# Three 256-column matmuls in place of a 512 and a 256 for channel-major weight tiles, with a one-step eviction

## The chip, the cores and the metric

The kernel runs on one core of one Trainium2 chip. The metric is device microseconds of one execution; the time of a kernel is the median of its runs. Engines are named as in the profile: PE is TensorE's matmul, PEld its weight load, DVE VectorE, ACT ScalarE, POOL GpSimd, SP SyncE, which issues the transfers.

## The reference

One decoder layer over 256 positions of width 2048, in float32:

```python
h = rmsnorm(x, norm1_g)
qkv, z, b_raw, a_raw, u_raw, v_raw, ga_raw, gb_raw = split(h @ w_in)
qkv = silu(causal_dwconv(qkv, dn_conv_w))          # 4 taps, along time, per channel
y_a = rmsnorm(gated_delta_rule(q, k, v, ...)) * silu(z)
y_b = gelu(u_raw) * spatial_mix(layernorm(gelu(v_raw)))
x = x + (sigmoid(ga_raw) * (y_a @ w_branch_a) + sigmoid(gb_raw) * (y_b @ w_branch_b)) @ w_out
h2 = rmsnorm(x, norm2_g)
gate = causal_dwconv(h2 @ ffn_w_gate, ffn_conv_w) + ffn_conv_b   # 3 taps
x = x + (silu(gate) * (h2 @ ffn_w_up)) @ ffn_w_down               # D_FF = 5632
return rmsnorm(x, final_norm_g)
```

## The kernel before

All products run in float32r, split for precision. A weight block arrives in SBUF by one transfer of 1 MB (`w_raw`), and `split` makes two float32r tiles of it: ACT casts the block to `w_hi` (L123), and DVE subtracts to get `w_lo`, the remainder (L124). The activations are split the same way and kept side by side in one tile: columns 0 to 255 are the high part of the 256 positions, columns 256 to 511 the low part. A product is hi x hi + lo x hi + hi x lo; the smallest term is left out.

There are two kinds of product. In the token-major kind (`tok_steps`, L157 to L159, and the down projection, L863 to L865) the weights stream as the moving operand, and the activations are loaded as stationary weights: three matmuls per tile, of 512 columns (346 and 348 in ps_u). In the channel-major kind (`chan_group`, L186 and L189) the weight tile is the stationary operand, 128 x 128, and the 256 positions move, so that channels lie on partitions and the causal convolution can run along the free axis. It is used in two stages: the six groups of qkv (ps_qkv) and the 22 groups of gate and up in the feed-forward part (ps_gu). A group is 512 output channels, that is, four row blocks in four PSUM banks (two from pool acc, two from aux, each pool with four banks, so that two groups fit), accumulated over 16 blocks of the inner dimension. The weights come in chunks of two inner blocks, through a ring of four buffers for each of hi and lo; a chunk is 8 weight tiles.

`chan_evict` takes a pair of row blocks out of PSUM into `dst` (`pre` in qkv, `gu` in gate-up), adds the two halves and multiplies by `rrow`, the reciprocal root of the normalisation for each position. Behind it come the convolution (ACT and DVE), the silu (ACT) and, in gate-up, the product with up into `y_f` on POOL.

A scheduler of the framework orders each engine's instructions, and puts work of one stage in between that of another where it expects room. So at the end of the qkv stage, PE already runs matmuls of the gates (ps_gate), and the preparation of the delta rule starts: ps_g on PE, exponentials on ACT (L489 to L495), the product g_r on POOL (L498), which ps_gr on PE (L500) waits for. g_r waits for the last silu of v (`v_t`, L454). ACT loads a table when it changes from silu to the exponential or back.

Of the kernel before, what the change touches and what calls it, by code (L numbers as in the profile page):

```python
# [9 lines left out]
F32 = mybir.dt.float32  # L10
F32R = mybir.dt.float32r
AF = mybir.ActivationFunctionType
ALU = mybir.AluOpType
# [3 lines left out]
P = 128  # L17
D = 2048
T = 256
NT = T // P  # L20
NK = D // P
# [77 lines left out]
def decoder_kernel(ctx: ExitStack, tc: tile.TileContext, a: dict):  # L99
    nc = tc.nc  # L100
# [7 lines left out]
    acc = ctx.enter_context(tc.tile_pool(name="acc", bufs=4, space=PSUM))  # L108
    aux = ctx.enter_context(tc.tile_pool(name="aux", bufs=4, space=PSUM))

    def bank(pool, name):
        return pool.tile([P, 512], F32, name=name, tag="bank")
# [14 lines left out]
    def source(name, g):  # L127

        cols = GROUPS[name]
        return a["w_" + name], sum(n for _, n in cols[:g]), cols[g][1]  # L130

    def stream(src, n_k, before=None):

        flat, start, width = src
        for k0 in range(0, n_k, 4):
            raw = wraw.tile([P, 4, 512], F32, name="w_raw", tag="raw")
            at = P * (start * n_k + k0 * width)
            block = flat[at : at + 4 * P * width].rearrange("(p k n) -> p k n", p=P, n=width)

            n, m = (4, 2) if not before else (2, 2) if k0 else (1, 1)  # L140
            for j in range(0, 4, n):
                if before:
                    before(k0 + j, n)
                nc.sync.dma_start(raw[:, j : j + n, 0:width], block[:, j : j + n, :])
            for j in range(0, 4, m):
                yield k0 + j, m, *split(raw[:, j : j + m, 0:width], [P, m, 512], "w")

    def tok_steps(x, src, n_k, name, before=None):

        ps = [bank(acc, f"{name}{t}")[:, 0 : src[2]] for t in range(NT)]  # L150
        for k0, n, hi, lo in stream(src, n_k, before):
            for t in range(NT):
                for j in range(n):
                    k = k0 + j
                    xh = x[:, k, t * P : (t + 1) * P]
                    xl = x[:, k, T + t * P : T + (t + 1) * P]
                    nc.tensor.matmul(ps[t], lhsT=xh, rhs=hi[:, j, :], start=(k == 0), stop=False)  # L157
                    nc.tensor.matmul(ps[t], lhsT=xh, rhs=lo[:, j, :], start=False, stop=False)  # L158
                    nc.tensor.matmul(  # L159
                        ps[t], lhsT=xl, rhs=hi[:, j, :], start=False, stop=(k == n_k - 1)  # L160
                    )
            yield
        return ps

    def finish(steps):

        while True:
            try:
                next(steps)
            except StopIteration as e:  # L170
                return e.value

    def tok_group(*args, **kw):
        return finish(tok_steps(*args, **kw))

    def chan_group(x, src, name):


        ps = [bank(pool, name) for pool in (acc, acc, aux, aux)]
        for k0, n, hi, lo in stream(src, NK):  # L180
            for m in range(4):
                ms = slice(m * P, (m + 1) * P)
                for j in range(n):
                    k = k0 + j
                    xk = x[k // 8][:, k % 8, :] if isinstance(x, list) else x[:, k, :]
                    nc.tensor.matmul(  # L186
                        ps[m], lhsT=hi[:, j, ms], rhs=xk, start=(k == 0), stop=(k == NK - 1), skip_group_check=True
                    )
                    nc.tensor.matmul(  # L189
                        ps[m][:, 0:T], lhsT=lo[:, j, ms], rhs=xk[:, 0:T], start=False, stop=(k == NK - 1),  # L190
                        skip_group_check=True,
                    )
        return ps

    def chan_evict(pool, dst, ps):

        lo = pool.tile([P, 2, T], F32, name="ev_lo", tag="ev_lo")
        for i in range(2):
            nc.scalar.copy(lo[:, i, :], ps[i][:, T:])
            nc.vector.tensor_tensor(dst[:, i, :], ps[i][:, 0:T], lo[:, i, :], op=ALU.add)  # L200
        nc.gpsimd.tensor_tensor(dst, dst, bc(rrow, 1, 2), op=ALU.mult)  # L201

    def split_stat(dst_hi, dst_lo, src, scale=None):

# [55 lines left out]
    def bc(ap, axis, n):  # L260

        shape = list(ap.shape)
        shape.insert(axis, n)
        return ap.unsqueeze(axis).broadcast_to(shape)

    def rsqrt_small(dst, src, scale):

        n = src.shape[-1]
        v = small.tile([P, n], F32, name="rs_v", tag=f"rs_v{n}")
        nc.vector.tensor_scalar(v, src, scalar1=scale, scalar2=EPS, op0=ALU.mult, op1=ALU.add)  # L270
        nc.gpsimd.tensor_tensor(dst, v, neg_half[:, 0:n], op=ALU.pow)

    def row_broadcast(dst, col):

        ps = bank(aux, "ps_row")
        for t in range(NT):
            dg = small.tile([P, P], F32, name="dg", tag="dg")
            nc.vector.tensor_scalar(
                dg, cm["ident"], scalar1=col[:, t : t + 1], scalar2=None, op0=ALU.mult
            )  # L280
            nc.tensor.matmul(ps[:, t * P : (t + 1) * P], lhsT=cm["ones"], rhs=dg, start=True, stop=True)
        nc.scalar.copy(dst, ps[:, 0:T])
# [14 lines left out]
    rrow = const.tile([P, T], F32, name="rrow")  # L297
# [11 lines left out]
    with tc.tile_pool(name="sg", bufs=1) as sg:  # L309
# [28 lines left out]
        for c, (start, width) in enumerate(GROUPS["bau"]):  # L338
            ps = tok_group(x_h, source("bau", c), NK, "ps_u_")
# [77 lines left out]
    def qkv_group(col):  # L417

        ps = chan_group(x_h, source("qkv", col // 512), "ps_qkv")
        for b in range(2):  # L420
            pre = tmp.tile([P, 2, 4 + T], F32, name="pre", tag="pre")
            nc.gpsimd.memset(pre[:, :, 0:4], 0.0)
            chan_evict(tmp, pre[:, :, 4:], ps[2 * b : 2 * b + 2])
            for m in range(2):
                ct = col // P + 2 * b + m
                cv = tmp.tile([P, T], F32, name="cv", tag="cv")
                nc.scalar.activation(cv, pre[:, m, 4:], AF.Copy, scale=cw[:, 4 * ct + 3 : 4 * ct + 4])
                for j in range(3):
                    nc.vector.scalar_tensor_tensor(
                        cv, pre[:, m, 1 + j : 1 + j + T], cw[:, 4 * ct + j : 4 * ct + j + 1], cv,  # L430
                        op0=ALU.mult, op1=ALU.add,
                    )
                yield ct, cv
# [360 lines left out]
    tmp = ctx.enter_context(tc.tile_pool(name="p3t", bufs=2))  # L794
# [4 lines left out]
    for c in range(4):  # L799
        cs = slice(512 * c, 512 * (c + 1))  # L800
        ps = finish(wo_steps if c == 0 else tok_steps(x_m, source("out", c), NK, "ps_wo"))
# [4 lines left out]
        for q in range(2):  # L806
            ps_t = bank(aux, "ps_x2t")
            for i in range(2):
                for t in range(NT):
                    k = 4 * c + 2 * q + i  # L810
# [3 lines left out]
            for i in range(2):  # L814
                k = 4 * c + 2 * q + i
# [4 lines left out]
    for f in range(0, NF, 2):  # L820
        ps = chan_group(x_h2, source("gu", f // 2), "ps_gu")
        if f == 0:
            rstd2 = const.tile([P, NT], F32, name="rstd2")
            s2 = const.tile([P, NT], F32, name="s2")
            nc.vector.tensor_reduce(s2, ss2, axis=AX.X, op=ALU.add)
            rsqrt_small(rstd2, s2, 1.0 / D)
            row_broadcast(rrow, rstd2)
        for i in range(2):
            ff = f + i
            gu = tmp.tile([P, 2, 384], F32, name="gu", tag="gu")[:, :, 0 : 4 + T]  # L830
            nc.gpsimd.memset(gu[:, 0, 0:4], 0.0)
            chan_evict(tmp, gu[:, :, 4:], ps[i::2])
            cv = tmp.tile([P, T], F32, name="f_cv", tag="f_cv")
            nc.scalar.activation(
                cv, gu[:, 0, 4:], AF.Identity, scale=fcw[:, 3 * ff + 2 : 3 * ff + 3], bias=fcb[:, ff : ff + 1]
            )
            for j in range(2):
                nc.vector.scalar_tensor_tensor(
                    cv, gu[:, 0, 2 + j : 2 + j + T], fcw[:, 3 * ff + j : 3 * ff + j + 1], cv,
                    op0=ALU.mult, op1=ALU.add,  # L840
                )
            nc.scalar.activation(cv, cv, AF.Silu)
            nc.gpsimd.tensor_tensor(y_f[ff // 32][:, ff % 32, :], cv, gu[:, 1, 4:], op=ALU.mult)
# [39 lines left out]
    for t in range(NT):  # L883
        for c in range(4):

            for h in range(1 if c < 3 else 2):
                w = 512 if c < 3 else 256
                lo = 512 * c + w * h
# [82 lines left out]
```

## Time and profile before

| | us |
|---|---|
| median of 3 runs | 1443.18 (1441.46 to 1444.53) |
| profiled execution | 1441.32 |
| its span, first to last instruction | 1439.6 |
| PE busy | 1418.4 |
| DVE, ACT, POOL busy | 898.0, 719.1, 241.9 |
| qkv stage, first to last start of a ps_qkv matmul | 106.2 to 241.2 |
| gate-up stage, the same of ps_gu | 701.7 to 1191.6 |

Rows of the trace give a start in microseconds from the span's start, a duration, the engine, the line of the kernel and the operands. Rows of groups give the count after x, then the total busy time and the mean of one in ns, then the idle time of the engine just before them. Rows of waits give the total, the number of times and the longest. A matmul's recorded duration includes its way through the array, so that the pace of a stream is read from starts, not from durations.

### The profile page before, as it was taken

The numbers are of one execution on the slowest core, as the hardware profiler recorded it, in microseconds if no ns is written. First come the engines' busy times: TensorE is split into PE (matmuls) and PEld (weight loads), VectorE is DVE, ScalarE is ACT, GpSimd is POOL, SyncE is SP. The second block draws the span as 40 slices with busy tenths as digits, with TensorE's granted clock in tenths as the row PEclk, the third lists the DMA queues.
The fourth block names the chain that finished last, engine by engine and source line by source line (L and its number), as shares of the span: only waits on it lengthen the run. The fifth ranks groups of instructions, "written<-read, shape, count | busy, mean of one in ns | idle before, by whom it ended". The sixth has DMA issues, their size and how long they took to land.

```text
span 1439.6 us, 19488 instructions
## 1 busy us (share of the span) xinstructions
PE 1418.4 (99%) x7762; PEld 1211.0 (84%) x7762; DVE 898.0 (62%) x1109; ACT 719.1 (50%) x975; POOL 241.9 (17%) x218
## 2 busy tenths in 40 slices
PE   8999999998999999999999999999999999999997
PEld 6898888786888888888888888888888888888886
DVE  6756777687465644655566766766657666555555
ACT  6556556543333444445455554555545545444444
POOL 0401111422010300300022322312213221000002
PEclk9999999999999999999999999999999999999999
DMA  9664555444433455575555555555555555555552
GB/s 339 207 225 155 211 196 176 146 150 172 147 124 140 150 201 197 183 263 184 188 185 187 193 181 200 178 202 182 199 182 198 181 201 183 198 196 187 201 188 105
DMA packets 46044, 269.19 MB, mean 187 GB/s; under 512 B 4736, under 2 KB 12672, under 8 KB 15616
## 3 DMA queue, kind: packets, MB, share of 16 engines
q1 hardware_dynamic: 45664, 266.89, 52.5%
q8 instruction: 61, 1.00, 0.3%
q10 hardware_dynamic: 288, 1.05, 0.2%
q14 instruction: 31, 0.25, 0.1%
HBM read 265.83 MB, written 2.10 MB: 186 GB/s over the span
## 4 chain that ended last, share of the span: by engine, by line
PE 94%; DVE 3%; POOL 1%; issue 1%; DMA 0%; ACT 0%; SPq 0%; POOLq 0%; DVEq 0%; ACTq 0%
PE ps_gu L186 22%; PE ps_gu L189 12%; PE ps_qkv L186 6%; PE ps_dn L865 5%; PE ps_dn L864 5%; PE ps_dn L863 5%; PE ps_gate L157 3%; PE ps_gate L158 3%; PE ps_gate L159 3%; PE ps_qkv L189 3%; PE ps_wo L157 2%; PE ps_wo L159 2%; PE ps_wo L158 2%; PE ps_br L157 2%; PE ps_br L159 2%; PE ps_br L158 2%
## 5 line engine op out<-in xcount | busy, mean ns | idle before, releaser
L124 DVE TENSOR_TENSOR w_lo<-w_raw,w_hi 128x1024 fp32r<-128x1024 f32 (+3 forms) x410 | 536.4, 1313 | 360.6 <-ACT w_hi L123 358.5
L123 ACT CAST w_hi<-w_raw 128x1024 fp32r<-128x1024 f32 (+3 forms) x410 | 422.0, 1031 | 461.7 <-PE ps_gu L186 156.9
L186 PE MATMUL ps_gu<-x_h,w_hi 128*128 128x512 f32 x1408 | 488.9, 392 | 0.0
L189 PE MATMUL ps_gu<-x_h,w_lo 128*128 128x256 f32 x1408 | 394.4, 280 | 0.0
L186 PEld LDWEIGHTS ps_gu<-x_h,w_hi 128*128 128x128 f32 x1408 | 263.4, 187 | 57.9
L189 PEld LDWEIGHTS ps_gu<-x_h,w_lo 128*128 128x128 f32 x1408 | 266.2, 189 | 0.0
L124 DVE TENSOR_TENSOR w_lo<-wd_raw,w_hi 128x1024 fp32r<-128x1024 f32 x84 | 104.1, 1239 | 105.2 <-ACT w_hi L123 105.2
L123 ACT CAST w_hi<-wd_raw 128x1024 fp32r<-128x1024 f32 x84 | 88.6, 1055 | 120.3 <-PE ps_dn L865 113.0
L186 PE MATMUL ps_qkv<-x_h,w_hi 128*128 128x512 f32 x384 | 133.6, 394 | 0.0
L864 PE MATMUL ps_dn<-w_lo,y_s 128*128 128x512 f32 x336 | 130.8, 389 | 0.0
L865 PE MATMUL ps_dn<-w_hi,y_s 128*128 128x512 f32 x336 | 130.8, 389 | 0.0
L863 PE MATMUL ps_dn<-w_hi,y_s 128*128 128x512 f32 x336 | 130.7, 389 | 0.0
L201 POOL TENSOR_TENSOR gu<-gu,rrow 128x512 f32<-128x512 f32 x44 | 61.4, 1395 | 337.7 <-DVE gu L200 316.2
L189 PE MATMUL ps_qkv<-x_h,w_lo 128*128 128x256 f32 x384 | 106.5, 278 | 0.0
L158 PE MATMUL ps_gate<-w_lo,x_h 128*128 128x512 f32 x256 | 100.6, 393 | 4.8 <-DVE w_lo L124 4.8
L157 PE MATMUL ps_gate<-w_hi,x_h 128*128 128x512 f32 x256 | 101.8, 398 | 0.0
L159 PE MATMUL ps_gate<-w_hi,x_h 128*128 128x512 f32 x256 | 100.4, 392 | 0.0
L186 PEld LDWEIGHTS ps_qkv<-x_h,w_hi 128*128 128x128 f32 x384 | 72.0, 188 | 16.5
L864 PEld LDWEIGHTS ps_dn<-w_lo,y_s 128*128 128x128 f32 x336 | 63.1, 188 | 13.2
L863 PEld LDWEIGHTS ps_dn<-w_hi,y_s 128*128 128x128 f32 x336 | 63.1, 188 | 13.1
L865 PEld LDWEIGHTS ps_dn<-w_hi,y_s 128*128 128x128 f32 x336 | 63.1, 188 | 13.0
L189 PEld LDWEIGHTS ps_qkv<-x_h,w_lo 128*128 128x128 f32 x384 | 72.1, 188 | 0.2
(258 smaller groups left out, 1826.6 us busy)
## 6 DMA issues: line engine op xcount, KB each, us to landing
w_raw<-in_w_gu SPq DMA_DIRECT2D x88, 1024.0 KB, 4.8
wd_raw<-in_ffn_w_down SPq DMA_DIRECT2D x44, 1024.0 KB, 4.8
w_raw<-in_w_qkv SPq DMA_DIRECT2D x24, 1024.0 KB, 4.8
w_raw<-in_w_gb SPq DMA_DIRECT2D x16, 1024.0 KB, 4.8
w_raw<-in_w_ga SPq DMA_DIRECT2D x16, 1024.0 KB, 4.8
w_raw<-in_w_out SPq DMA_DIRECT2D x16, 1024.0 KB, 4.8
w_raw<-in_w_branch_b SPq DMA_DIRECT2D x8, 1024.0 KB, 4.8
w_raw<-in_w_z SPq DMA_DIRECT2D x8, 1024.0 KB, 4.8
```

What stands on the lines that cost most here:

```text
L123: nc.scalar.copy(hi, raw)
L124: nc.vector.tensor_tensor(lo, raw, f32(hi), op=ALU.subtract)
L157: nc.tensor.matmul(ps[t], lhsT=xh, rhs=hi[:, j, :], start=(k == 0), stop=False)
L158: nc.tensor.matmul(ps[t], lhsT=xh, rhs=lo[:, j, :], start=False, stop=False)
L159: nc.tensor.matmul(ps[t], lhsT=xl, rhs=hi[:, j, :], start=False, stop=(k == n_k - 1))
L186: nc.tensor.matmul(ps[m], lhsT=hi[:, j, ms], rhs=xk, start=(k == 0), stop=(k == NK - 1), skip_group_check=True)
L189: nc.tensor.matmul(ps[m][:, 0:T], lhsT=lo[:, j, ms], rhs=xk[:, 0:T], start=False, stop=(k == NK - 1), skip_group_check=True,)
L201: nc.gpsimd.tensor_tensor(dst, dst, bc(rrow, 1, 2), op=ALU.mult)
L863: nc.tensor.matmul(o, lhsT=yh, rhs=hi[:, cs], start=(k == 0), stop=False)
L864: nc.tensor.matmul(o, lhsT=yh, rhs=lo[:, cs], start=False, stop=False)
L865: nc.tensor.matmul(o, lhsT=yl, rhs=hi[:, cs], start=False, stop=(k == NF - 1))
```

## The change

For each weight tile, `chan_group` issued two matmuls: hi against all 512 columns of the activations into a whole bank, and lo against the 256 high columns into the bank's first half. Now it issues three of 256 columns, all into the first half: hi against the high columns, lo against the high columns, hi against the low columns. The two halves of the bank no longer have to be added, so `chan_evict` is one product of the bank's first half with `rrow` on DVE; the copy on ACT and the product on POOL go.

```diff
-        ps = [bank(pool, name) for pool in (acc, acc, aux, aux)]
+        ps = [bank(pool, name)[:, 0:T] for pool in (acc, acc, aux, aux)]
...
-                    nc.tensor.matmul(
-                        ps[m], lhsT=hi[:, j, ms], rhs=xk, start=(k == 0), stop=(k == NK - 1), skip_group_check=True
-                    )
-                    nc.tensor.matmul(
-                        ps[m][:, 0:T], lhsT=lo[:, j, ms], rhs=xk[:, 0:T], start=False, stop=(k == NK - 1),
-                        skip_group_check=True,
-                    )
+                    nc.tensor.matmul(ps[m], lhsT=hi[:, j, ms], rhs=xk[:, 0:T], start=(k == 0), stop=False)
+                    nc.tensor.matmul(ps[m], lhsT=lo[:, j, ms], rhs=xk[:, 0:T], start=False, stop=False)
+                    nc.tensor.matmul(ps[m], lhsT=hi[:, j, ms], rhs=xk[:, T:], start=False, stop=(k == NK - 1))
...
-    def chan_evict(pool, dst, ps):
-
-        lo = pool.tile([P, 2, T], F32, name="ev_lo", tag="ev_lo")
+    def chan_evict(dst, ps):
+
         for i in range(2):
-            nc.scalar.copy(lo[:, i, :], ps[i][:, T:])
-            nc.vector.tensor_tensor(dst[:, i, :], ps[i][:, 0:T], lo[:, i, :], op=ALU.add)
-        nc.gpsimd.tensor_tensor(dst, dst, bc(rrow, 1, 2), op=ALU.mult)
+            nc.vector.tensor_tensor(dst[:, i, :], ps[i], rrow, op=ALU.mult)
```

The order of PE in a gate-up group, before. A row gives the line, the operation, output <- inputs with the numbers of the buffers, and the output's shape; each pair stands twice, for the two inner blocks of a chunk, and is shown once:

```order
L186 MATMUL ps_gu_6032<-x_h20_5235,w_hi_6038 128x512
L189 MATMUL ps_gu_6032<-x_h20_5235,w_lo_6039 128x256
...
L186 MATMUL ps_gu_6033<-x_h20_5235,w_hi_6038 128x512
L189 MATMUL ps_gu_6033<-x_h20_5235,w_lo_6039 128x256
...
L186 MATMUL ps_gu_6034<-x_h20_5235,w_hi_6038 128x512
L189 MATMUL ps_gu_6034<-x_h20_5235,w_lo_6039 128x256
```

And now, at the same place:

```order
L185 MATMUL ps_gu_6424<-x_h20_5571,w_hi_6430 128x256
L186 MATMUL ps_gu_6424<-x_h20_5571,w_lo_6431 128x256
L187 MATMUL ps_gu_6424<-x_h20_5571,w_hi_6430 128x256
...
L185 MATMUL ps_gu_6425<-x_h20_5571,w_hi_6430 128x256
L186 MATMUL ps_gu_6425<-x_h20_5571,w_lo_6431 128x256
L187 MATMUL ps_gu_6425<-x_h20_5571,w_hi_6430 128x256
```

The same weight tile w_hi is used by the first and the third matmul, with w_lo between them, so that it is loaded twice.

The change also moves work at the end of the qkv stage, since the scheduler expects other times. ACT's order there before, from the last copy of an eviction to the last silu of v:

```order
L199 COPY ev_lo<-ps_qkv 128x256
L489 ACT_TABLE_LOAD
L489 ACTIVATE egd<-egd 128x8
L491 ACTIVATE beg<-gs 128x8
L493 ACTIVATE egx<-gs 128x8
L495 ACTIVATE egl<-gs 128x16
L123 CAST w_hi<-w_raw 128x1024
L454 ACT_TABLE_LOAD
L454 ACTIVATE v_t<-cv 128x2x128 x2
L427 ACTIVATE cv<-pre,par 128x256 x2
L123 CAST w_hi<-w_raw 128x1024 x2
L454 ACTIVATE v_t<-cv 128x2x128 x2
```

And now (L446 is the silu of v, L481 to L487 the exponentials, L419 the first tap of the convolution):

```order
L446 ACTIVATE v_t<-cv 128x2x128
L481 ACT_TABLE_LOAD
L481 ACTIVATE egd<-egd 128x8
L446 ACT_TABLE_LOAD
L446 ACTIVATE v_t<-cv 128x2x128
L419 ACTIVATE cv<-pre,par 128x256
L483 ACT_TABLE_LOAD
L483 ACTIVATE beg<-gs 128x8
L485 ACTIVATE egx<-gs 128x8
L446 ACT_TABLE_LOAD
L446 ACTIVATE v_t<-cv 128x2x128
L487 ACT_TABLE_LOAD
```

Silu and exponential now alternate, so that four table loads stand ahead of the last silu of v where two stood; the casts that stood among them now stand ahead of this piece or behind it. On PE, the number of ps_gate matmuls between ps_g and the first ps_gr, which waits for g_r, goes from 47 to 52. The order of the transfers does not change.

More of the change, by code (lines that the diff above doesn't have):

```diff
@@ L422, in qkv_group @@
             nc.gpsimd.memset(pre[:, :, 0:4], 0.0)
-            chan_evict(tmp, pre[:, :, 4:], ps[2 * b : 2 * b + 2])
+            chan_evict(pre[:, :, 4:], ps[2 * b : 2 * b + 2])
             for m in range(2):
@@ L831, in decoder_kernel @@
             nc.gpsimd.memset(gu[:, 0, 0:4], 0.0)
-            chan_evict(tmp, gu[:, :, 4:], ps[i::2])
+            chan_evict(gu[:, :, 4:], ps[i::2])
             cv = tmp.tile([P, T], F32, name="f_cv", tag="f_cv")
```

## Prediction

> **What bounds the kernel now.** I read the page first, then PE's waits, the table by stages, PE's timeline inside three stages, and last the chain and ACT's timeline at the end of the qkv stage. The page gives each engine's busy share and the shares of the chain that ended last:
>
> ```profile
> span 1439.6 us, 19488 instructions
> PE 1418.4 (99%) x7762; PEld 1211.0 (84%) x7762; DVE 898.0 (62%) x1109; ACT 719.1 (50%) x975; POOL 241.9 (17%) x218
> ...
> PE 94%; DVE 3%; POOL 1%; issue 1%; DMA 0%; ACT 0%; SPq 0%; POOLq 0%; DVEq 0%; ACTq 0%
> ```
>
> PE is the bound: 94% of the chain is matmuls, and each of the 7762 matmul records has a weight load (PEld) of its own. A busy PE says nothing of its pace, so I looked at what it waits for, over the whole span:
>
> ```profile
> PE ps_gate L158 <- DVE w_lo L124: 4.8, 2, 4.4
> PE ps_u L158 <- DVE w_lo L124: 2.4, 3, 0.8
> ...
> PE ps_gr L500 <- POOL g_r L498: 1.8, 1, 1.8
> ...
> ```
>
> The three rows left out are of ps_wup and ps_vg, at the start; none is a matmul of ps_qkv, ps_gu or ps_dn. In the two stages that change, PE waits neither for weights nor for banks, so the eviction's arithmetic is hidden, and what counts is how fast PE gets through the matmuls. Only ps_gr, just behind the qkv stage, depends on anything that the eviction feeds.
>
> **The pace of PE, by stage.** A table by stages over the gate-up loop (first row) and the down projection (second), with its columns: window, sum, PE busy (records), PEld, DVE, ACT, POOL, granted clock, share of the transfers, GB/s:
>
> ```profile
> 730.00:1180.00 450.00, 450.00 (x2598) 396.81 (x2597) 298.40 (x331) 240.72 (x331) 118.92 (x125) 1.00 0.54 189
> 1205.00:1405.00 200.00, 200.00 (x884) 165.61 (x883) 101.97 (x111) 88.82 (x110) 0.00 (x0) 1.00 0.55 194
> ```
>
> Both are full at clock 1.00. To get exact paces I take the first and last matmul that start inside each window, from PE's timeline: the pairs of the gate-up loop, the 512-wide matmuls of the down projection, and the 346-wide ones of ps_u in the window below them.
>
> ```profile
> 730.26 0.39 PE L186 MATMUL ps_gu<-x_h,w_hi 128*128 128x512 f32 x1
> 1179.88 0.39 PE L186 MATMUL ps_gu<-x_h,w_hi 128*128 128x512 f32 x1
> ...
> 1205.09 0.39 PE L865 MATMUL ps_dn<-w_hi,y_s 128*128 128x512 f32 x1
> 1404.78 0.39 PE L864 MATMUL ps_dn<-w_lo,y_s 128*128 128x512 f32 x1
> ...
> 73.00:86.00 13.00, 13.00 (x84) 13.00 (x83) 5.99 (x7) 7.19 (x12) 0.00 (x0) 1.00 0.72 220
> 73.02 0.33 PE L157 MATMUL ps_u<-w_hi,x_h 128*128 128x346 f32 x1
> 85.94 0.32 PE L157 MATMUL ps_u<-w_hi,x_h 128*128 128x346 f32 x1
> ```
>
> Each count includes two matmuls begun before the window. So 2596 starts in the gate-up window are 1298 pairs: (1179.88 - 730.26)/1297 = 346.7 ns a pair. The down projection has 882 starts: (1404.78 - 1205.09)/881 = 226.7 ns for 512 columns. ps_u has 82: (85.94 - 73.02)/81 = 159.5 ns for 346.
>
> Let one matmul cost a fixed a, and b for each column. Then a + 512 b = 226.7, and the pair, two matmuls with 768 columns, gives 2a + 768 b = 346.7. One and a half times the first is 1.5a + 768 b = 340.0, so 0.5 a = 6.7: **a = 13.3 ns, b = 0.4167 ns**. The third width tests it: 13.3 + 346 x 0.4167 = 157.5, against 159.5 measured (a would be 15.3). A pace by columns alone would want 153.2 for 346 columns and 340.0 for the pair, and both rows refuse it. Every matmul with its own weights costs 13 to 15 ns beside its columns.
>
> **Part one: two matmuls become three.** Columns stay at 768 for each weight tile: 512 + 256 before, 3 x 256 now. Weight loads rise from two to three, because hi is loaded twice with lo between. A triple should take 3 x (13.3 + 256 x 0.4167) = 360.0 ns, 13.3 more than the pair. The groups on the page give the counts, 1408 pairs of ps_gu and 384 of ps_qkv:
>
> ```profile
> L189 PE MATMUL ps_gu<-x_h,w_lo 128*128 128x256 f32 x1408 | 394.4, 280 | 0.0
> L189 PE MATMUL ps_qkv<-x_h,w_lo 128*128 128x256 f32 x384 | 106.5, 278 | 0.0
> ```
>
> 1792 x 13.3 = **23.9 us**, 18.8 in gate-up and 5.1 in qkv, all on the path since both stages run on PE alone. Bounds: 15.3 ns from ps_u gives 27.4 us; the lower bound is from the rows of the first rival.
>
> Does the load still hide beneath a matmul of 256 columns? Before, this happens once in a pair; now it happens every time. The timeline of one pair, with its loads:
>
> ```profile
> 950.28 0.28 PE L189 MATMUL ps_gu<-x_h,w_lo 128*128 128x256 f32 x1
> 950.28 0.19 PEld L186 LDWEIGHTS ps_gu<-x_h,w_hi 128*128 128x128 f32 x1
> 950.39 0.39 PE L186 MATMUL ps_gu<-x_h,w_hi 128*128 128x512 f32 x1
> 950.39 0.19 PEld L189 LDWEIGHTS ps_gu<-x_h,w_lo 128*128 128x128 f32 x1
> 950.62 0.28 PE L189 MATMUL ps_gu<-x_h,w_lo 128*128 128x256 f32 x1
> ```
>
> The load starts with the narrow matmul, and the next load starts 0.11 us later, though a load is recorded as 0.19 us long. So loads overlap, a spacing of 0.11 us is possible, and the triple asks for 0.12. The pair's sum, in which one load lies under 256 columns, shows no exposed time. I take nothing for it; the margin is thin, hence a rival below. "TensorE: Matmul & The Clock Gate", section "LDWEIGHTS (loading the stationary operand)", of the Trainium skill puts a load at its columns over 1.2, which would be an estimated 107 ns for 128, as long as 256 columns stream: the trace's 0.11 agrees, and by it too the load is just hidden. The sum is the same either way.
>
> **Part two: the eviction.** For each of 56 pairs of row blocks, two ACT copies, two DVE additions and a POOL product become two DVE products:
>
> ```profile
> L201 POOL TENSOR_TENSOR gu<-gu,rrow 128x512 f32<-128x512 f32 x44 | 61.4, 1395 | 337.7 <-DVE gu L200 316.2 <-ACT rrow L282 21.4
> L199 ACT COPY ev_lo<-ps_gu 128x256 f32<-128x256 f32 x88 | 32.0, 364 | 11.3 <-PE ps_gu L189 11.3
> L200 DVE TENSOR_TENSOR gu<-ps_gu,ev_lo 128x256 f32<-128x256 f32 x88 | 33.9, 416 | 0.0
> ...
> L201 POOL TENSOR_TENSOR pre<-pre,rrow 128x512 f32<-128x512 f32 x12 | 20.0, 1670 | 121.3 <-DVE pre L200 121.3
> L199 ACT COPY ev_lo<-ps_qkv 128x256 f32<-128x256 f32 x24 | 8.8, 365 | 3.0 <-PE ps_qkv L189 2.8
> ```
>
> ACT loses 32.0 + 8.8 = 41 us and POOL 61.4 + 20.0 = 81 us. DVE keeps its count; the product reads PSUM and SBUF like the addition, so 416 ns each. On the path this is worth nothing in either stage: PE hides it, and its list of waits has no row there.
>
> The product now waits for PE itself, where the addition waited for ACT. Queued behind it on DVE are the next w_lo splits, for which PE waits. Their cover: the casts ahead of them wait for PE to free buffers,
>
> ```profile
> ACT w_hi L123 <- PE ps_gu L186: 162.2, 129, 1.8
> DVE w_lo L124 <- ACT w_hi L123: 463.6, 364, 3.7
> 950.52 1.05 ACT L123 CAST w_hi<-w_raw 128x1024 fp32r<-128x1024 f32 x1 [0.29 <-ACT ev_lo L199]
> 951.60 2.17 DVE L124 TENSOR_TENSOR w_lo<-w_raw,w_hi 128x1024 fp32r<-128x1024 f32 x1
> ```
>
> so splitting runs a ring of four buffers ahead. A chunk is 8 pairs, 8 x 0.347 = 2.8 us; three chunks of lead are 8.3 us, less a cast (1.05) and a slow split (2.17): some 5 us of cover against a wait of a fraction of a microsecond. I take 0. A slower PE makes the cover longer, and the weight transfers (busy share 0.54) are asked for less often.
>
> **Part three: the end of the qkv stage.** The chain of waits there, and ACT's timeline:
>
> ```profile
> 241.51 1.01 PE ps_g L483 x10
> 250.87 1.06 ACT w_hi L123
> 251.92 0.63 ACT v_t L454 x2
> 252.68 2.40 POOL g_r L498
> 255.12 1.12 PE ps_gr L500 x2
> ...
> 244.21 1.28 ACT L489 ACT_TABLE_LOAD   x1
> 246.98 1.28 ACT L454 ACT_TABLE_LOAD   x1
> 252.94 0.39 PE L158 MATMUL ps_gate<-w_lo,x_h 128*128 128x512 f32 x1
> ```
>
> PE's last gate matmul ends its columns at 252.94 + 0.23 = 253.17, and ps_gr starts at 255.12: 1.9 us lost. POOL's g_r comes 13.6 us after the qkv matmuls end (241.51), behind the last v_t on ACT. In the new order PE has 52 gate matmuls before ps_gr, not 47, and arrives 5 x 0.227 = 1.1 us later. On ACT, ahead of the last v_t, two casts (2.1 us) and a copy (0.36) go, and two table loads (2.56) come: g_r is as late as before, within a microsecond or two. I take a gain of 1.1 us; ends +1.9 (the wait gone) and -2 (two table loads in the way). The 4.8 us for w_lo at ps_gate come later, in the delta rule, where the order shifts by single splits only; I take nothing for them.
>
> **Sum.** The profiled execution took 1441.3 us, 1.7 beyond its span of 1439.6. 1441.3 + 23.9 - 1.1 = 1464.1. The median of the three runs, 1443.2, is 1.9 above that execution: **1466 us**, 1.6% slower.
>
> **Rivals.** *The fixed cost is paid mainly by the wide matmul.* In the rows above, hi starts 0.11 us after lo starts (950.28 to 950.39), and lo 0.23 after hi (950.39 to 950.62). With 230 of the pair's 346.7 ns on the wide one, the narrow one costs 116.7, where a = 13.3 asks for 120. Read literally, a triple is 350.1 ns, only 3.4 more: 1792 x 3.4 = 6.1 us, less 1.1, so 1448, and starts rounded to 0.01 us leave that open by a few us. Against it: the down projection's uniform stream takes 226.7 for 512 columns, not 230, so the 3 ns look like an early recorded start of the hi matmul, which must cancel in a uniform stream. By the same skill page, section "Back-to-back issue gap", a warm matmul has a gap of only 2.5 ns beyond its columns, which would give an estimated 4.5 us for the extra 1792; the rows here, 13.3 and 15.3, disagree with it for these operands. I give this rival 10%.
>
> *Loads do not hide in a row.* If only alternate loads can overlap, as the rows strictly show, two loads take 0.11 + 0.19 = 0.30 us, a triple 0.45, and the kernel loses 1792 x 0.10 = 186 us: about 1630. It decides as soon as a load holds its port for over 120 ns. Against it stand eight transposes in a row, each with a load, at 0.87/8 = 109 ns:
>
> ```profile
> 586.43 0.87 PE ps_tc L288 x8
> ```
>
> Those are plain fp32 loads. 4%, or 5% with milder forms.
>
> *Faster: the fixed cost comes from changing width.* If PE pays only when the width or the PSUM window changes from one matmul to the next, the uniform triple costs 3 x 106.7 = 320 ns, 26.7 less than the pair, and 1792 x 26.7 = 47.8 us go: 1394. It decides once a falls below 8.9 ns, where 3a is 26.7. The uniform streams of 512 and 346 columns pay the 13 ns as well. 2%.
>
> **Numbers.** The forecast has 83%. Its own range takes a from 12 ns (towards the first rival's 116.7 - 106.7 = 10) to 15.3, so 21.5 to 27.4 us, and the boundary from +1.9 to -2: 1463 to 1473. I give 1459 to 1473, four more below for the first rival in part; the rivals as such stay outside. Within 0.2% (2.9 us, about what a measurement of this kernel can tell from no change) lies part of the first rival: 4%. Faster 3%, the last rival and a little of the first; slower 93%.
>
> **What would show it.** In the changed profile the gate-up loop has a triple every 360 ns, 120 between starts, and lasts about 19 us longer; qkv lasts 5 us longer; the down projection keeps 226.7. ACT is down by 41 us and POOL by 81, with nothing for it at the end. PE has no new wait in either stage. I am wrong if starts are 116 apart or less, or if loads come more than 120 ns apart.

## The result and the profile after

| | before | after |
|---|---|---|
| median, us | 1442.32 (1440.88 to 1444.53) | 1468.8 (1467.93 to 1470.94) |
| profiled execution, span | 1441.32, 1439.6 | 1468.83, 1467.1 |
| ratio of the times | | 1.0184 (1.0169 to 1.0199) |

The changed kernel is 1.84% slower, 27.5 us by the two spans and 26.5 by the medians. The prediction said 1466, in a range of 1459 to 1473. The page of the changed kernel, its engines and the shares of the chain that ended last:

```profile
span 1467.1 us, 22807 instructions
PE 1443.4 (98%) x9554; PEld 1311.6 (89%) x9554; DVE 864.3 (59%) x1109; ACT 680.8 (46%) x865; POOL 152.3 (10%) x162
...
PE 93%; DVE 4%; POOL 1%; ACT 1%; issue 1%; DMA 0%; SPq 0%; POOLq 0%; DVEq 0%; ACTq 0%
```

PE is still the bound, with 1792 matmuls and as many weight loads more, and 25.0 us more of busy time. ACT does 38 us less, POOL 90, DVE 34, and none of that shows at the end. The stage table for the same stretches of the gate-up loop and the down projection:

```profile
730.00:1180.00 450.00, 450.00 (x3753) 450.00 (x3752) 260.64 (x320) 201.11 (x243) 52.61 (x80) 1.00 0.52 183
1225.00:1425.00 200.00, 200.00 (x884) 165.62 (x883) 102.46 (x111) 89.02 (x111) 0.00 (x0) 1.00 0.55 192
```

3753 matmuls in 450 us are one every 119.9 ns, so a triple takes 360 ns. The loads now fill the whole stretch (450.00 of 450.00, from 396.81). The down projection has 884 records in 200 us, as before. PE's timeline in the gate-up loop shows the steady step:

```profile
899.74 0.28 PE L185 MATMUL ps_gu<-x_h,w_hi 128*128 128x256 f32 x1
899.86 0.28 PE L186 MATMUL ps_gu<-x_h,w_lo 128*128 128x256 f32 x1
899.98 0.28 PE L187 MATMUL ps_gu<-x_h,w_hi 128*128 128x256 f32 x1
```

The first and the last start of each stage divide the difference of the spans; the table below is worked out from the starts before rounding. Rows of the tiles, the changed kernel's here (name, count, shortest/median/longest duration in ns, first and last start):

```profile
L185 PE MATMUL ps_qkv<-x_h,w_hi x384: 279/283/364, 106.3 to 246.1; 128*128 128x256 f32 x192
L187 PE MATMUL ps_qkv<-x_h,w_hi x384: 278/283/366, 106.7 to 246.4; 128*128 128x256 f32 x192
L185 PE MATMUL ps_gu<-x_h,w_hi x1408: 277/283/365, 710.7 to 1218.7; 128*128 128x256 f32 x176
L187 PE MATMUL ps_gu<-x_h,w_hi x1408: 278/283/283, 711.0 to 1218.9; 128*128 128x256 f32 x176
```

| us | before | after | difference |
|---|---|---|---|
| before qkv | 106.2 | 106.3 | +0.1 |
| qkv | 135.0 | 140.0 | +5.0 |
| from qkv to gate-up | 460.4 | 464.4 | +4.0 |
| gate-up | 489.9 | 508.2 | +18.3 |
| behind gate-up | 248.1 | 248.2 | +0.1 |

The two stages give 23.3 us. The 4.0 us between them, where no matmul was changed, are the surprise. PE's waits of the changed kernel:

```profile
PE ps_gate L158 <- DVE w_lo L124: 8.0, 3, 4.4
...
PE ps_gr L492 <- POOL g_r L490: 0.6, 1, 0.6
```

The wait for g_r has shrunk from 1.8 to 0.6 us, but PE now waits 8.0 us for split weights at ps_gate instead of 4.8, three times instead of twice. Where the third wait lies shows in the timelines of PE, DVE and ACT behind the qkv stage; a bracket gives the idle time ahead and who ended it:

```profile
270.69 0.33 PE L539 MATMUL ps_kk<-kq 128*64 128x64 f32 x2
274.20 0.79 PE L158 MATMUL ps_gate<-w_lo,x_h 128*128 128x512 f32 x1 [3.19 <-DVE w_lo L124]
274.79 0.63 PE L159 MATMUL ps_gate<-w_hi,x_h 128*128 128x512 f32 x1
275.22 0.63 PE L157 MATMUL ps_gate<-w_hi,x_h 128*128 128x512 f32 x1
...
271.12 0.69 DVE L518 TENSOR_REDUCE ssx<-sq_qk 128x4 f32<-128x512 f32 x1
271.84 0.69 DVE L519 TENSOR_TENSOR k_d<-ps_kt,egd 64x512 f32<-64x512 f32 x1
272.92 1.23 DVE L124 TENSOR_TENSOR w_lo<-w_raw,w_hi 128x1024 fp32r<-128x1024 f32 x1
...
264.65 0.63 ACT L499 ACTIVATE low<-low 128x512 f32<-128x512 f32 x1 [1.29 <-POOL low L497]
266.99 0.63 ACT L500 ACTIVATE att<-att 128x512 f32<-128x512 f32 x1 [1.71 <-POOL att L498]
267.53 1.07 ACT L517 ACTIVATE sq_qk<-ps_kt 128x512 f32<-128x512 f32 x2
268.49 1.05 ACT L123 CAST w_hi<-w_raw 128x1024 fp32r<-128x1024 f32 x1
```

The chunk that PE needs next is cast at 268.49, behind two exponentials that wait for POOL, and split at 272.92, behind the last reductions (ssx) and products (k_d) of the delta rule's preparation. In the kernel before, the same pieces stood so:

```profile
257.39 1.05 ACT L123 CAST w_hi<-w_raw 128x1024 fp32r<-128x1024 f32 x1
259.76 0.63 ACT L507 ACTIVATE low<-low 128x512 f32<-128x512 f32 x1
...
257.42 0.69 DVE L526 TENSOR_REDUCE ssx<-sq_qk 128x4 f32<-128x512 f32 x1 [0.43 <-ACT sq_qk L525]
258.02 0.67 DVE L527 TENSOR_TENSOR k_d<-ps_kt,egd 64x512 f32<-64x512 f32 x1
258.62 1.21 DVE L124 TENSOR_TENSOR w_lo<-w_raw,w_hi 128x1024 fp32r<-128x1024 f32 x1
```

There the cast stands ahead of both exponentials, and the split behind the first ssx and k_d; in the changed kernel ten instructions of DVE, from an ssx at 268.14 to a copy at 272.72, stand between this split and the one ahead of it, where three stood before. The cast was done at 269.54, so that a split right behind it would have been done at 270.8, before PE ran out of work at 271.0: it is DVE's order that makes PE wait. The wait costs 3.2 us, and something more: behind it the matmuls start 0.43 us apart, not 0.227. The granted clock is the last but two column of the table of stretches:

```profile
273.90:277.40 3.50, 3.20 (x8) 2.52 (x9) 1.46 (x3) 0.91 (x2) 3.09 (x1) 0.51 0.54 192
352.40:355.90 3.50, 3.50 (x11) 2.69 (x9) 2.64 (x3) 0.00 (x0) 0.00 (x0) 0.51 0.54 187
```

Twice PE is at half clock for 3.4 us, each time behind a wait. The second stands in the trace of before too (at 343.2, behind the wait of 4.4 us); the first is new. PE still waits in its first 0.3 us (273.9 to 274.20), and the other 3.1 us at half speed lose 1.6. So 3.2 for the wait, 1.6 for the clock, less 1.2 won at ps_gr: 3.6 of the 4.0 us. The other 0.4 is spread over steps too short to be listed as waits and stays open. The Trainium skill ("TensorE: Matmul & The Clock Gate", section "What's actually happening") tells of a PE that falls to half its clock after at least one idle window of some 3.4 us. The trace agrees in the length of the pieces, 3.4 us, but here a wait of 3.2 us, shorter than such a window, was enough; the last section shows how much of a window a wait has to fill.

### The profile page after: what moved, and what is told of

It is laid out like the page before. It is cut to its first block, busy times and chain, and to the rows that moved or that the text cites. A ratio compares the mean times of both kernels' runs of the same rounds, so it can differ in the third digit from the quotient of the medians.

```text
span 1467.1 us, 22807 instructions
## 1 busy us (share of the span) xinstructions
PE 1443.4 (98%) x9554; PEld 1311.6 (89%) x9554; DVE 864.3 (59%) x1109; ACT 680.8 (46%) x865; POOL 152.3 (10%) x162
## 4 chain that ended last, share of the span: by engine, by line
PE 93%; DVE 4%; POOL 1%; ACT 1%; issue 1%; DMA 0%; SPq 0%; POOLq 0%; DVEq 0%; ACTq 0%
PE ps_gu L186 12%; PE ps_gu L185 12%; PE ps_gu L187 12%; PE ps_dn L857 5%; PE ps_dn L855 5%; PE ps_dn L856 5%; PE ps_qkv L187 3%; PE ps_qkv L185 3%; PE ps_qkv L186 3%; PE ps_gate L158 3%; PE ps_gate L157 3%; PE ps_gate L159 3%; PE ps_wo L157 2%; PE ps_wo L158 2%; PE ps_wo L159 2%; PE ps_br L157 2%
## 5 line engine op out<-in xcount | busy, mean ns | idle before, releaser
L124 DVE TENSOR_TENSOR w_lo<-w_raw,w_hi 128x1024 fp32r<-128x1024 f32 (+3 forms) x410 | 503.7, 1233 | 384.4 <-ACT w_hi L123 383.7
L185 PE MATMUL ps_gu<-x_h,w_hi 128*128 128x256 f32 x1408 | 398.6, 283 | 0.0
L186 PE MATMUL ps_gu<-x_h,w_lo 128*128 128x256 f32 x1408 | 398.5, 283 | 0.0
L187 PE MATMUL ps_gu<-x_h,w_hi 128*128 128x256 f32 x1408 | 398.4, 283 | 0.0
L186 PEld LDWEIGHTS ps_gu<-x_h,w_lo 128*128 128x128 f32 x1408 | 270.3, 192 | 0.0
L185 PEld LDWEIGHTS ps_gu<-x_h,w_hi 128*128 128x128 f32 x1408 | 270.3, 192 | 0.0
L187 PEld LDWEIGHTS ps_gu<-x_h,w_hi 128*128 128x128 f32 x1408 | 270.3, 192 | 0.0
L187 PE MATMUL ps_qkv<-x_h,w_hi 128*128 128x256 f32 x384 | 108.9, 284 | 0.0
L185 PE MATMUL ps_qkv<-x_h,w_hi 128*128 128x256 f32 x384 | 108.8, 284 | 0.0
L835 POOL TENSOR_TENSOR y_f<-f_cv,gu 128x256 f32<-128x256 f32 x44 | 53.4, 1213 | 450.4 <-ACT f_cv L834 450.4
L857 PEld LDWEIGHTS ps_dn<-w_hi,y_s 128*128 128x128 f32 x336 | 63.1, 188 | 13.1
```

The lines of the kernel that those rows point to most:

```text
L124: nc.vector.tensor_tensor(lo, raw, f32(hi), op=ALU.subtract)
L185: nc.tensor.matmul(ps[m], lhsT=hi[:, j, ms], rhs=xk[:, 0:T], start=(k == 0), stop=False)
L186: nc.tensor.matmul(ps[m], lhsT=lo[:, j, ms], rhs=xk[:, 0:T], start=False, stop=False)
L187: nc.tensor.matmul(ps[m], lhsT=hi[:, j, ms], rhs=xk[:, T:], start=False, stop=(k == NK - 1))
L857: nc.tensor.matmul(o, lhsT=yl, rhs=hi[:, cs], start=False, stop=(k == NF - 1))
```

## Experiments

Two questions: is it the number of matmuls alone that costs the two stages their time, and what is the fixed cost of 13.3 ns? And do the 4.0 us come from where a split stands? Times of a kernel are compared with the kernel before, run on the same chip; stages are read as in the table above, each from one profiled execution. The expectations have the stretch from qkv to gate-up from rounded starts, 460.3 us before and 464.3 after.

**The matmuls alone.** Three matmuls of 256 columns, but the third goes into the bank's second half, so that the old eviction stays, and with it, nearly, the order at the end of qkv (two table loads ahead of the last silu of v, and 48 matmuls of the gates ahead of ps_gr, where before had 47).

```diff
-    nc.tensor.matmul(ps[m], lhsT=hi[:, j, ms], rhs=xk, start=(k == 0), ...)
-    nc.tensor.matmul(ps[m][:, 0:T], lhsT=lo[:, j, ms], rhs=xk[:, 0:T], start=False, ...)
+    for h, wt, st, cols in ((0, hi, k == 0, xk[:, 0:T]), (0, lo, False, xk[:, 0:T]), (1, hi, False, xk[:, T:])):
+        nc.tensor.matmul(ps[m][:, h * T : (h + 1) * T], lhsT=wt[:, j, ms], rhs=cols, start=st, ...)
```

> Three matmuls of 256 columns, but the third into the second half of the bank, and the eviction of before (ACT copy, DVE addition, POOL product). Theory (13.3 ns for each matmul with its own weights, and 3.9 us more from the new order at the end of qkv, which comes from the new eviction): starts 120 ns apart, gate-up 18.3 us and qkv 5.0 us longer than before, the stretch from the end of qkv to the start of gate-up within 1 us of the 460.3 us of before, so about 23 us more than before: 1465 to 1466. Rival (the 3.9 us also come from the matmuls, since PE is later against the other engines): stretch 464, 1469.

**The eviction alone.** The pair of 512 and 256 stays, and the eviction is the new one, on the bank's first half.

```diff
-            nc.scalar.copy(lo[:, i, :], ps[i][:, T:])
-            nc.vector.tensor_tensor(dst[:, i, :], ps[i][:, 0:T], lo[:, i, :], op=ALU.add)
-        nc.gpsimd.tensor_tensor(dst, dst, bc(rrow, 1, 2), op=ALU.mult)
+            nc.vector.tensor_tensor(dst[:, i, :], ps[i][:, 0:T], rrow, op=ALU.mult)
```

> Two matmuls of 512 and 256 columns as before, and the new eviction, of the first half of the bank alone (hi x low columns is computed and left out of the result). Theory: pair stays at 346.7 ns; the order at the end of qkv is that of the changed kernel (four table loads ahead of the last silu, the split behind the norms), so the stretch from the end of qkv to gate-up is 462 to 465 us against 460.3 of before, and the kernel is 2 to 5 us slower than before. Rival (the lighter eviction helps, and only the slower matmuls upset the order's fit): stretch 460 or less, 0 to 2 us faster than before.

| us | median (before) | ratio | qkv | between | gate-up |
|---|---|---|---|---|---|
| before | | | 135.0 | 460.4 | 489.9 |
| matmuls alone | 1465.97 (1443.72) | 1.0158 (1.0141 to 1.0175) | 140.0 | 460.7 | 508.2 |
| eviction alone | 1445.49 (1443.72) | 1.0010 (0.9999 to 1.0022) | 137.5 | 463.9 | 489.9 |
| both: after | 1468.8 (1442.32) | 1.0184 (1.0169 to 1.0199) | 140.0 | 464.4 | 508.2 |

In gate-up the parts add up, and between the stages nearly so (0.2 and 3.4 us against 4.0). The matmuls bring 5.0 and 18.3 us and leave the stretch between as it was; the eviction brings 3.4 us there and nothing in gate-up. PE's waits, first with the matmuls alone and then with the eviction alone, name the place:

```profile
PE ps_gate L158 <- DVE w_lo L124: 4.8, 2, 4.4
...
PE ps_gr L498 <- POOL g_r L496: 1.3, 1, 1.3
```

```profile
PE ps_gate L158 <- DVE w_lo L124: 7.2, 4, 4.4
```

With the eviction alone, PE's wait for g_r is gone from the list, the wait for w_lo is 2.4 us longer, and one of 0.4 us for w_hi is new. The waits alone come to only 1.0 us more than before; another 1.7 us is lost at half clock, behind a wait of 2.2 us that ends at 269.7:

```profile
270.30:273.70 3.40, 3.40 (x10) 2.66 (x9) 1.67 (x3) 0.00 (x0) 2.78 (x1) 0.50 0.49 157
```

That is 2.7 of the 3.4 us. The order is not that of the changed kernel in every place: 47 matmuls of the gates, not 52, stand ahead of ps_gr. With the matmuls alone two differences nearly cancel: 0.5 us less of waiting at ps_gr, and half clock for 6.8 us, not 3.4, behind the wait of 4.4.

One thing was not expected: with the eviction alone qkv took 2.5 us longer (last section); the changed kernel's qkv is no longer than that of the matmuls alone. The whole kernel was 1.8 us slower by the medians, a little under the 2 to 5 expected, and its ratio, +0.10%, is not told apart from no change by its interval; the stages tell more than the total.

**The split's place.** The changed kernel, with one number changed: the delta rule's preparation gives way for three chunks instead of two before it goes on, so that the splits of the stream come earlier in DVE's order.

```diff
-        yield 2
+        yield 3
```

> The changed kernel, with one chunk more of the gates written between the first and the second step of the delta rule's preparation. It puts the weight split that PE waited 3.2 us for ahead of the second pair of norms on DVE and ACT. Theory (that split's place in the order costs the 3.2 us): PE's wait for w_lo at ps_gate there falls below 1 us and the stretch from the end of qkv to gate-up falls from 464.3 to 460 to 462 us, the kernel to 1465 to 1467. Rival (the delta rule's own chain on DVE sets the stretch, and the wait only moves to the solve): stretch 463 to 465, no change.

The median was 1466.24 (before 1443.72), ratio 1.0161 (1.0146 to 1.0176), and the stretch between the stages 461.9 us instead of 464.4. PE's waits:

```profile
PE ps_br L158 <- DVE w_lo L124: 4.4, 1, 4.4
...
PE ps_gate L158 <- DVE w_lo L124: 0.8, 2, 0.4
```

The wait of 3.2 us is gone; the one of 4.4 us now meets ps_br. Of the 4.0 us, 2.5 came back. Most of the rest, 1.1 us, is in the clock:

```profile
351.70:358.50 6.80, 5.63 (x13) 4.52 (x14) 4.52 (x4) 0.53 (x1) 0.00 (x0) 0.50 0.49 175
```

Behind the same wait of 4.4 us the half clock lasted 6.8 us here, not 3.4. So the place of the split is shown to be the cause of the new wait: it is 3.2 us in the changed kernel and in the five other experiments built on it, and 0.4 here. The gain in time is less sure, since the stretch between the stages differs among those six, from 462.9 to 466.9 us, by the half clock alone (last section), and the intervals of the two ratios overlap a little (1.0146 to 1.0176 here, 1.0169 to 1.0199 for the changed kernel).

**The same edit in the kernel before**, as a control: if it were a gain by itself, the last experiment would show nothing of the new order.

> The kernel before with one chunk more of the gates between the first two steps of the delta rule's preparation, the edit of the third experiment without the change itself. Theory (in the changed kernel the edit repaired a split that stood too late; before, no split stood late): stretch from the end of qkv to gate-up within 2 us of 460.3, 1442 to 1446, no faster. Rival (the edit is good by itself, and what the third experiment gained has nothing to do with the order that the change brought): stretch 457 to 458, 2 to 3 us faster than before.

1443.39 against 1442.91, ratio 1.0005 (0.9992 to 1.0018): no difference, and the stretch between the stages took 461.3 us against 460.4. The edit gains where the new order had lost, and gains nothing in the kernel before.

**Half the stationary columns.** The changed kernel, with 64 of 128 columns of each weight tile loaded and used in all inner blocks but the first. The moving columns stay at 256.

```diff
+                    w = P if k == 0 else 64
+                    ws = slice(m * P, m * P + w)
+                    o = ps[m][0:w]
...
-                    nc.tensor.matmul(ps[m], lhsT=hi[:, j, ms], rhs=xk[:, 0:T], start=(k == 0), stop=False)
...
+                    nc.tensor.matmul(o, lhsT=hi[:, j, ws], rhs=xk[:, 0:T], start=(k == 0), stop=False, skip_group_check=True)
...
```

> The changed kernel, with only the first 64 of the 128 columns of each stationary tile loaded for all inner blocks but the first; the other 64 channels of each row block keep the sum of the first block alone. Loads become half as wide, and the moving columns stay 256. Theory A (13.3 ns is fixed for each matmul): starts stay 120 ns apart. Theory B (it is the tail of a load of 128 columns that does not hide): 113 ns apart or less, gate-up about 30 us shorter.

**Three quarters of them**, w = 96, the same way.

> The changed kernel, with only 96 of the 128 stationary columns loaded and multiplied in every inner block but the first, in qkv and gate-up, all in float32r; the other output rows miss their sums. Theory (the fixed cost is a share of the weight load and grows with its columns, 7.2 ns at 64 and 13.3 at 128): about 10.3 ns, starts 117.0 apart in the gate-up stage, some 3158 matmul records in a window of 370 us, recorded loads about 165 ns (between 137 and 192). Rival (two steps only: a load of up to half the array is quick, a larger one pays the whole): starts 120.0 apart or 113.8 apart, no value between.

The stretch from 730 to 1100 us of the gate-up loop, and the weight loads of one line: first the changed kernel, then 96 columns, then 64.

```profile
730.00:1100.00 370.00, 370.00 (x3086) 370.00 (x3085) 213.40 (x261) 164.90 (x199) 42.03 (x64) 1.00 0.52 183
...
L186 PEld LDWEIGHTS ps_gu<-x_h,w_lo 128*128 128x128 f32 x1408 | 270.3, 192 | 0.0
```

```profile
730.00:1100.00 370.00, 370.00 (x3188) 370.00 (x3186) 221.27 (x273) 173.02 (x207) 44.72 (x68) 1.00 0.54 190
...
L189 PEld LDWEIGHTS ps_gu<-x_h,w_lo 128*96 128x96 f32 (+1 forms) x1408 | 228.6, 162 | 0.0
```

```profile
730.00:1100.00 370.00, 370.00 (x3254) 370.00 (x3252) 226.03 (x279) 176.78 (x210) 44.73 (x68) 1.00 0.55 194
...
L189 PEld LDWEIGHTS ps_gu<-x_h,w_lo 128*64 128x64 f32 (+1 forms) x1408 | 193.4, 137 | 0.0
```

370 us over the counts: 119.9, 116.1 and 113.7 ns a matmul. One inner block in 16 is still loaded whole; away from these blocks the step is 120.0, 116.0 and 113.3. Less the 106.7 ns of 256 columns, the fixed cost is **13.3, 9.3 and 6.7 ns**. It falls with the stationary columns, and 96 lies between the others, 1 ns under the 10.3 expected and on neither of the rival's two steps. (With 96 the single steps are uneven, 112 to 121 ns in a pattern of five, so that 116.0 is a mean.) So the cost is not one of the change from one matmul to the next. That it is the load's is argued, not shown: the edit narrows the load and the rows that the matmul writes together. For the load speaks that bfloat16 (below) writes all 128 rows at a fixed cost of 2.4 ns. The whole kernels took 1448.82 and 1435.49 us in single runs.

**Another order of the three.** hi, hi, lo instead of hi, lo, hi, so that two matmuls in a row have the same stationary tile.

> The changed kernel with the three matmuls of a weight tile in the order hi, hi, lo: the second loads the weights that the first has just loaded. Theory (the cost stands with every load, whatever it holds): starts stay 120.0 ns apart for all three. Rival (it is paid when the weights change): the second hi starts 107 to 109 ns after the first, gate-up 15 to 18 us shorter.

Starts stayed 120.0 ns apart, all three alike, and gate-up took 508.2 us: a repeated tile is loaded again and pays again. The down projection had shown it before the change: its first two matmuls of three have the same stationary tile (L863 and L864), and all three start 226.7 ns apart. The single run took 1471.27 us. Its stretch between the stages was 466.9 us, with the waits of the changed kernel (8.1 us for w_lo) but with half clock for twice as long behind each of them:

```profile
273.30:280.10 6.80, 6.00 (x36) 4.59 (x38) 4.00 (x8) 2.76 (x4) 4.26 (x2) 0.50 0.43 154
351.80:358.70 6.90, 5.52 (x13) 4.36 (x14) 4.74 (x5) 0.42 (x1) 0.00 (x0) 0.51 0.49 173
```

**Another type.** The gate-up products in bfloat16: the high and low parts of weights and activations are kept in that type, which rounds more coarsely. Once in the changed kernel, and once in the kernel before with its pair.

```diff
+    def split16(raw, shape, tag):
+        hi, lo = (wsp.tile([...], BF16, ...) for n in ("hi", "lo"))
+        nc.scalar.copy(hi, raw)
+        nc.vector.tensor_tensor(lo, raw, hi, op=ALU.subtract)
...
-    x_h2 = [xpool.tile([P, 8, 2 * T], F32R, ...) ...]
+    x_h2 = [xpool.tile([P, 8, 4 * T], BF16, ...)[..., 0 : 2 * T] ...]
```

> The changed kernel with the gate-up products in bfloat16 in place of float32r (hi and lo of weights and activations rounded to bfloat16); qkv as it was. Theory (the 13.3 ns are the unhidden part of a float32r load, a tenth of a nanosecond for each of its columns, and a load of half the bytes hides): starts in gate-up are 109 ns apart, 2.5 beyond the columns as the plain fp32 transposes have, gate-up takes 1408 x 3 x 10.8 = 46 us less than in the changed kernel, 1423. Rival (the cost is of a load of 128 columns whatever its type): 120 ns and 1468.

> The kernel before, with the gate-up products in bfloat16 and the two matmuls of 512 and 256 columns. Theory: a pair takes 320 + 2 x 2.5 = 325 ns against 346.7, gate-up 1408 x 21.7 = 30.5 us less than before, 1413; and three matmuls would then cost only 2.5 ns more than two for each tile. Rival: 346.7 and 1443.

The three matmuls took 1425.07 us (before 1442.91), ratio 0.9871 (0.9843 to 0.9898); the pair took **1412.95**, ratio 0.9785 (0.9761 to 0.9810). Both beat both kernels. The stretch and a load of the three in bfloat16:

```profile
730.00:1100.00 370.00, 370.00 (x3392) 331.67 (x3391) 234.32 (x290) 182.90 (x219) 46.76 (x72) 1.00 0.57 201
...
L197 PEld LDWEIGHTS <-w_lo 128*128 128x128 bf16 x1408 | 137.8, 98 | 16.0
```

370/3392 = 109.1 ns: a fixed cost of 2.4, where float32r pays 13.3. (The transposes that the expectation names are no measure of it: they start 109 ns apart with 128 moving columns, not 256.) The gap that the Trainium skill gives ("TensorE: Matmul & The Clock Gate", section "Back-to-back issue gap"), 2.5 ns, is what bfloat16 shows here, and not what float32r does. The three matmuls lose little against the pair in this type: gate-up took 462.5 and 458.8 us, 3.7 us apart, for 1408 matmuls more (1408 x 2.4 = 3.4); in float32r it was 18.3. The other 9 us between the two kernels are qkv, still in float32r, and the stretch behind it (140.0 + 464.5 against 135.0 + 460.4).

**Half the columns in bfloat16.** Is bfloat16 cheap because its whole load is quick?

> The changed kernel with the gate-up products in bfloat16, and there only 64 of the 128 stationary columns in every inner block but the first; the other output rows miss their sums. Theory one (the fixed cost follows the columns of the load, whatever the type): 64 columns cost no more than 128, so starts of at most 109.1 ns and recorded loads below 98 ns. Theory two (bfloat16 is cheap only because a full 128-column load of that type is done on a quicker path): half the columns lose that path, loads are recorded at about 137 ns as with 64 float32r columns, and starts are about 113.8 ns apart, so that the smaller load makes the stage 4% slower, by some 20 us.

Neither theory came out whole. In the gate-up loop the mean is 113.8 ns (3252 matmuls in the same 370 us), and the stage takes 482.2 us, as the second one asks; the timeline shows that this mean is of two things. Long stretches run at 109 ns; where the first inner block of a group, with all 128 columns, stands beside blocks of 64, it goes like this:

```profile
909.41 0.27 PE L201 MATMUL ps_gu<-x_h,w_hi 128*64 128x256 bf16 x1
909.62 0.28 PE L199 MATMUL ps_gu<-x_h,w_hi 128*128 128x256 bf16 x1
909.74 0.27 PE L200 MATMUL ps_gu<-x_h,w_lo 128*128 128x256 bf16 x1
909.85 0.27 PE L201 MATMUL ps_gu<-x_h,w_hi 128*128 128x256 bf16 x1
910.05 0.30 PE L199 MATMUL ps_gu<-x_h,w_hi 128*64 128x256 bf16 x1
```

Each change between a load of 128 and one of 64 columns costs about 0.1 us (0.21 and 0.20 from start to start instead of 0.11), eight times in a group. Away from them 64 columns go at 109.2 ns, as 128 do, though their load is recorded as longer, 110 ns against 98. So in bfloat16 the fixed cost is 2.5 ns for either size. The columns matter in float32r, where loads are recorded at 137 to 192 ns. Why that type leaves 0.1 ns for each stationary column in the open (13.3/128, 6.7/64), under 256 moving columns as under 512, stays open; bfloat16 changes the moving operand too, so that these runs don't say which of the two makes the difference.

## Why the prediction was right

- *What bounds the kernel*: PE without waits in the two stages. It held: no row of ps_qkv, ps_gu or ps_dn stands among the waits of the changed kernel.
- *The pace of PE*: 13.3 ns beside 0.4167 ns a column, from three streams before. It held to the digit: 120.0 between starts, 360.0 a triple, and 226.7 untouched in the down projection.
- *Part one*: 23.9 us forecast, 23.3 measured (18.8 and 5.1 against 18.3 and 5.0), and 23.3 in the matmuls alone (22.3 by the medians, 1465.97 less 1443.72). Some 0.4 of the missing 0.6 is that the first gate-up group of before ran at a slower pace, 374.9 ns a pair in the mean with the other work that stands in it, while in another run of the same matmuls (the control above) it took 368.8: 64 pairs by 6.1 ns. The last section tells of that pace.
- *The load under 256 columns*: it hides as far as it did in the pair. A recorded load of 192 ns beside a step of 120 is no contradiction, since records of loads overlap. But the prediction was too easy in calling it hidden. The 0.11 us that it took for a load is the spacing of two starts, not the time of a load; and the 13.3 ns that it measured fall with the stationary columns (9.3 and 6.7 above), so that they are, as far as the runs show, the part that isn't hidden. The sum had them in a all the same.
- *Part two*: worth nothing on the path in both stages, and it is so, since the eviction alone left gate-up at 489.9. ACT lost 38 us for 41, since two table loads more (2.6 us) came back; POOL 90 for 81: its other products run shorter too (y_f 1213 ns for 1431). DVE's product takes 419 ns for the 416 forecast; DVE was to stay and lost 34, of which 33 are the splits of w_raw, 1233 ns for 1313 in the mean.
- *Part three* is the step that failed. A gain of 1.1 us was forecast, between +1.9 and -2; a loss of 4.0 was measured. The gain at ps_gr came, 1.2 us, and as forecast: g_r was as late as before, with ps_gr 13.8 us behind the last start of ps_qkv and 13.9 before. What failed is the sentence that took nothing for ps_gate "where the order shifts by single splits only". A single split that came behind ten other instructions on DVE, not three, was worth 3.2 us of PE, and PE's wait brought 1.6 us of half clock with it. The half clock behind the wait at ps_gate was there to be read in the trace of before.
- *The sum*: 23.9 - 1.1 = 22.8 forecast and 27.5 measured, on the profiled spans; the median came out 2.8 above the 1466, within the range. That it fell within is due to Part one alone. That 4.7 us too few became 2.8 is luck: the sum added 1.9 for a median above the profiled execution, and after the change the two are the same (1468.8 and 1468.83).
- *Rivals*: the narrow matmul at 116.7 is refuted by the 120.0. Loads that don't hide in a row are refuted by the same step, with two loads of hi in a row as well. The cost of a change of width is refuted by uniform triples at 13.3 each and, since the cost falls with the stationary columns at one and the same moving width, by 64 and 96 of them.

## What to carry to other kernels

Take the fixed cost of a matmul from two streams of different width in the kernel's own trace, and count matmuls with their own weights, not only columns: in float32r with 128 stationary columns one is worth 32 moving columns (13.3/0.4167). Where a change shifts an order, look at what stands ahead of each instruction that the bound engine waits for, one by one, and price a wait of some 3 us on PE with the half clock that can follow it. When a total cannot tell an edit from no change, time the stages: with the eviction alone 3.4 us stood out in one stage where the whole could not be told from before. Then look at the granted clock in each trace, since it alone moved that stage by up to 4 us between kernels of the same order.

## What the hardware showed beside this

The half clock behind a wait came in pieces of 3.4 or 6.8 us, never between. The same wait of 4.4 us had 3.4 us behind it in the changed kernel and 6.8 in four of the experiments. The wait of 3.2 us stands in six traces: four have 3.4 us at half clock behind it, one 6.8 (hi, hi, lo), and one none (half the columns in bfloat16). There the clock is 1.00 from 18.7 to 353.2 us, and the stretch between the stages took 462.9 us, 1.5 less than in the changed kernel.

What decides it can be read from the traces. In each of the twelve, every change of the clock stands a whole number of steps of 3.413 us behind the first one, which comes between 5.1 and 8.5 us from the start, at another place in each run: 337.9 us or 99 steps in the trace of before (5.2 to 343.2), 266.2 us or 78 steps in the changed kernel's (7.7 to 273.9). What counts is how much of one step PE's waits (idle times over 0.15 us) fill. Between the first change and 1400 us it is so: at full clock, every step with 66% or more was followed by half clock, and none with 48% or less; between 49 and 56% both occur. At half clock, a step with up to 13% was the last, and one with 23 to 51% was followed by another. The wait of 3.2 us filled 86% of one step in the changed kernel; in the trace without half clock it lay across two, with 48 and 46%. So these differences of 1.7 us are a matter of where a wait falls against the steps, which no edit here controls. This is read from twelve traces; no experiment was made to test it.

Near the start it is the same. PE waits there for its first weights, and in the control waits of 1.3 and 0.5 us filled 53% of a step: a piece of 3.4 us at half clock followed at 15.3 us, and qkv began 2.0 us later than in the kernel before, where waits of 0.8 and 0.5 filled 38% and no such piece stood.

Pairs of 512 and 256 have two steady paces. Two windows of qkv at clock 1.00, before first and the eviction alone below it:

```profile
110.00:240.00 130.00, 130.00 (x753) 113.65 (x753) 93.82 (x142) 78.55 (x126) 18.52 (x20) 1.00 0.53 187
```

```profile
110.00:240.00 130.00, 130.00 (x739) 112.91 (x739) 88.34 (x141) 72.09 (x104) 1.04 (x10) 1.00 0.53 187
```

753 and 739 matmuls in 130 us: 345 and 352 ns a pair, with the same instructions and no waits; exact starts of whole groups give 346.7 and 353.3. The first gate-up group of before ran at the slower pace in part (103 matmuls in the 18 us from 704, 106 in the 18 us from 730), then changed for good. It cost the eviction alone 2.5 us in qkv and would be 9 us in gate-up if it lasted. Uniform triples always ran at 120.0. What chooses the pace is open. It may be part of why the kernel before varies by 5 us between runs (1441.43 to 1446.35), where the matmuls alone vary by 1.2; but the clock is another part: in the set of runs beside the bfloat16 kernels the slowest run of before, 1447.98 us, had a mean clock of 0.993, and the fastest two, 1440.77 and 1440.92, had 0.998.
